# Second layer of a hybrid decoder: weights times values in fp32 on two column tiles of TensorE, instead of in high and low halves

## The chip, the cores and the metric

The kernel runs on one core of a Trainium2 chip. The metric is the device time of one execution in microseconds (us). The core's engines run side by side, each with its own instruction queue in program order: TensorE (PE; its weight loads are listed as PEld), VectorE (DVE), ScalarE (ACT), GpSimd (POOL) and SyncE (SP, which issues the DMAs here). L808 stands for line 808 of the kernel before.

## The reference

Two layers over x of shape (1, 1024, 1024) in float32. The first is differential attention, the second stick-breaking attention with 16 heads of 64; keys and values of the second are projected from the first one's output. The change touches the second layer's last einsum.

```python
def _stick_breaking(q, k, v):
    ...
        mask = kpos[None, :] < qpos[:, None]
        z = jnp.einsum('bhqd,bshd->bhqs', qb, k).astype(jnp.float32) * scale
        log_beta = jax.nn.log_sigmoid(z)
        log_1mb = jnp.where(mask, jax.nn.log_sigmoid(-z), 0.0)
        suffix = lax.cumsum(log_1mb, axis=3, reverse=True) - log_1mb
        a = jnp.where(mask, jnp.exp(log_beta + suffix), 0.0)
        return jnp.einsum('bhqs,bshe->bhqe', a.astype(v.dtype), v)

def _sb_layer(x, k, v, norm_g, w_in, w_out):
    ...
    o = _stick_breaking(q.reshape(b, s, SB_HEADS, SB_HEAD_DIM), k, v)
    o = o.reshape(b, s, SB_W) * jax.nn.silu(g)
    return x + o @ w_out
```

## The kernel before

Most matmuls take fp32r operands. To keep fp32 accuracy, an operand is split in a high half (an ACT copy to fp32r) and a low half (a DVE subtraction), and products of halves are summed in PSUM: three for the projections (`group`, L192 to L194) and for the scores (`scores`, L235).

The second layer works on eight pairs of heads. For a pair, `qkv_b` projects keys, values and queries with columns of both heads together; `v_done` (L745) has the values transposed back to rows (`v_rows`) and writes for each head j one 128 x 128 block for each block of 128 keys: 64 columns of high halves and 64 of low ones, in an order that puts the high ones on the columns of that head (L748 to L753). `unit_s_b` computes, for one block of 128 queries, the scores of both heads in two row tiles of the array (64 rows each, L235), evacuates them with ACT (L778), masks the diagonal block with POOL (L780) and runs the stick-breaking weights through ACT and DVE (L787 to L793), one row of queries for each partition.

`unit_t_b` takes a pair m of query blocks. Its steps (c, t) run over the heads c, and within a head over pairs t of key blocks, t = 0 to m. A step transposes the weights (`transposed`, L253: four 128 x 128 transposes into one PSUM tile `tr`, three in the last step t = m, where one block is masked away and its halves are zeroed by POOL, L267 and L268), splits the transposed weights in halves `th` (ACT, L269) and `tl` (DVE, L270), and multiplies each half of each of the two key blocks with the block of values (L808, L809), 256 query columns each. The sum of a head stands in PSUM in two sets of 64 partitions, weights times high values and weights times low ones. At the head's last step ACT copies the second set (L814) and DVE adds the first (L815) into `hd.o`. When both heads are through, `hd.done` counts the unit; `gate_mul` (L356) multiplies with the gate and stores to DRAM, and `OutProj` multiplies with the output weights.

The order of work: `run_layer` merges two lists of steps by the costs given with each step. The main list has the units of the current pair, with the T unit of one m behind the S unit of the next; the other has the projections of the next pair. The tile framework then orders the instructions of each engine by a simulated timeline (`schedule_with_timeline_sim=True`), so that instructions that would wait are passed by others that are ready. [...] SBUF tiles rotate by tags: three `th` and three `tl` in the pool of the whole kernel, four `v` of which a pair of the second layer holds two, eight score tiles `zl`, of which a unit with m of 2 or 3 holds four.

## Time and profile before

| | |
|---|---|
| median of 3 runs | 1470.85 us (1469.36 to 1471.21) |
| profiled execution | 1470.77 us |
| its span, first to last instruction | 1469.0 us |
| mean granted clock of TensorE | 0.98 |
| busy: PE, PEld, DVE, ACT, POOL | 96%, 81%, 74%, 64%, 20% |

The first layer and the first projections of the second run up to about 760 us, the second layer's attention with the projections of the following pairs from there to 1412 us, and the output projection closes the kernel. Busy times are those of one execution. Matmuls overlap in the pipeline, so the sum of their durations is more than PE's busy time; how far apart their starts are tells what one costs. [...]

### The profile page before, as it was taken

Reading aid. Unit: us, or ns where it says so; the run is one execution under the profiler, and the core shown is the slowest. Engines: PE = TensorE matmul, PEld = TensorE weight load, DVE = VectorE, ACT = ScalarE, POOL = GpSimd, SP = SyncE. Lnnn points to the kernel's source line nnn. Section 1 sums busy time; section 2 is a strip of 40 time slices with the busy share of each in tenths; the row PEclk is TensorE's granted clock in tenths of the full one; section 3 lists DMA queues with packets and bytes.
Section 4 is the critical chain, followed back from the end, with each engine's and each line's share of the span. In section 5 each row is a group of like instructions: output and inputs, shape, how many; then the busy total and the mean of one; then the engine's idle time right before and its main releaser. Section 6 shows DMA issues by size and latency. Waiting matters only on the chain.

```text
span 1469.0 us, 24503 instructions
## 1 busy us (share of the span) xinstructions
PE 1414.9 (96%) x8944; PEld 1192.0 (81%) x8944; DVE 1088.0 (74%) x2251; ACT 943.5 (64%) x1940; POOL 288.2 (20%) x545
## 2 busy tenths in 40 slices
PE   8999999999999999999999998998989999988899
PEld 7888888888888888799877776777867777767699
DVE  7586777777776867875458786887878788889952
ACT  7555566656565655453468777787777887788720
POOL 0111212121212112100011321322333242323100
PEclk9999999999999999999999998999999999998899
DMA  5111111111111124623111110111101010233412
GB/s 202 58 30 44 44 44 44 44 44 44 44 44 44 44 72 173 215 94 108 58 58 30 35 53 29 51 37 44 43 8 51 30 58 29 91 111 125 177 72 80
DMA packets 43113, 99.40 MB, mean 68 GB/s; under 512 B 4848, under 2 KB 6640, under 8 KB 41968
## 3 DMA queue, kind: packets, MB, share of 16 engines
q1 hardware_dynamic: 42992, 97.83, 19.4%
q8 instruction: 71, 1.16, 0.3%
q14 instruction: 50, 0.41, 0.1%
HBM read 74.74 MB, written 23.07 MB: 67 GB/s over the span
## 4 chain that ended last, share of the span: by engine, by line
PE 76%; DVE 12%; ACT 5%; issue 4%; DMA 1%; POOL 0%; SPq 0%; ACTq 0%; DVEq 0%; POOLq 0%
PE proj L192 18%; PE proj L193 18%; PE proj L194 17%; PE sc L235 8%; PE tr L263 5%; DVE u4k L792 5%; DVE u4k L790 2%; PE av L808 2%; PE av L809 2%; DVE tl L270 1%; PE av L638 1%; PE av L640 1%; PE av L639 1%; ACT u4k L788 1%; PE tr L571 1%
## 5 line engine op out<-in xcount | busy, mean ns | idle before, releaser
L192 PE MATMUL proj<-ah,w 128*128 128x512 f32 x768 | 310.3, 404 | 4.1 <-DVE kl L243 4.1
L193 PE MATMUL proj<-al,w 128*128 128x512 f32 x768 | 309.8, 403 | 0.0
L194 PE MATMUL proj<-ah,w 128*128 128x512 f32 x768 | 308.9, 402 | 0.0
L192 PE MATMUL proj<-w,ah 128*128 128x256 f32 x992 | 289.8, 292 | 4.0 <-DVE v L422 1.9
L194 PE MATMUL proj<-w,al 128*128 128x256 f32 x992 | 285.0, 287 | 0.0
L193 PE MATMUL proj<-w,ah 128*128 128x256 f32 x992 | 284.8, 287 | 0.0
L192 PEld LDWEIGHTS proj<-w,ah 128*128 128x128 f32 x992 | 191.3, 193 | 15.2 <-issue 5.8
L193 PEld LDWEIGHTS proj<-w,ah 128*128 128x128 f32 x992 | 191.5, 193 | 2.3 <-issue 1.0
L194 PEld LDWEIGHTS proj<-w,al 128*128 128x128 f32 x992 | 191.4, 193 | 1.5 <-issue 1.2
L192 PEld LDWEIGHTS proj<-ah,w 128*128 128x128 f32 x768 | 146.8, 191 | 39.8 <-DVE kl L243 5.6
L792 DVE TENSOR_TENSOR_SCAN u4k<-zl,u4k 128x768 f32<-128x768 f32 (+4 forms) x96 | 175.0, 1828 | 0.9
L193 PEld LDWEIGHTS proj<-al,w 128*128 128x128 f32 x768 | 146.9, 191 | 35.0 <-issue 7.1
L194 PEld LDWEIGHTS proj<-ah,w 128*128 128x128 f32 x768 | 146.5, 191 | 32.1 <-issue 3.0
L235 PE MATMUL sc<-kh,q 64*128 64x512 f32 (+2 forms) x768 | 159.7, 399 | 11.0 <-ACT zl L778 10.4
L270 DVE TENSOR_TENSOR tl<-tr,th 128x512 fp32r<-128x512 f32 (+1 forms) x240 | 146.5, 629 | 29.8 <-ACT th L269 28.6
L269 ACT ACTIVATE th<-tr 128x512 fp32r<-128x512 f32 (+1 forms) x240 | 126.2, 554 | 37.2 <-PE tr L263 32.1
L263 PE MATMUL tr<-ident,zl 128*128 128x128 f32 x864 | 131.0, 277 | 10.7 <-ACT zl L793 6.1
L793 ACT ACTIVATE zl<-u4k 128x768 f32<-128x768 f32 (+4 forms) x96 | 81.1, 846 | 87.9 <-DVE u4k L792 74.0
L161 ACT ACTIVATE w<-raw,cols 128x256 fp32r<-128x256 f32 x240 | 104.6, 502 | 46.6 <-PE proj L193 31.5
L780 POOL TENSOR_SCALAR_AFFINE_SELECT zl<-zl 128x128 f32<-128x128 f32 (+1 forms) x96 | 78.1, 819 | 278.9 <-ACT zl L778 278.7
L790 DVE SCALAR_TENSOR_TENSOR u4k<-zl,u4k 128x768 f32<-128x768 f32 (+4 forms) x96 | 95.5, 1007 | 44.9 <-ACT u4k L789 44.8
L235 PEld LDWEIGHTS sc<-kh,q 64*128 64x128 f32 x768 | 76.2, 186 | 62.7 <-issue 17.9
(148 smaller groups left out, 2630.7 us busy)
## 6 DMA issues: line engine op xcount, KB each, us to landing
raw<-in_w_kv_dram SPq DMA_DIRECT2D x32, 256.0 KB, 2.7
raw<-in_w_b_dram SPq DMA_DIRECT2D x32, 256.0 KB, 2.7
raw<-in_w_qk_dram SPq DMA_DIRECT2D x28, 256.0 KB, 2.7
raw<-in_w_vg_dram SPq DMA_DIRECT2D x28, 256.0 KB, 2.9
og_a<-o SPq DMA_DIRECT2D x28, 256.0 KB, 2.0
og_b<-o SPq DMA_DIRECT2D x28, 256.0 KB, 2.0
raw<-in_a_w_out_dram SPq DMA_DIRECT2D x26, 256.0 KB, 2.8
raw<-in_b_w_out_dram SPq DMA_DIRECT2D x26, 256.0 KB, 2.7
```

The lines of the kernel that those rows point to most:

```text
L161: act.activation(h[:, i], r, AF.Copy, scale=g)
L192: pe.matmul(box["p"], lh, rh, start=(j == 0), stop=False)
L193: pe.matmul(box["p"], lh, rl, start=False, stop=False)
L194: pe.matmul(box["p"], ll, rh, start=False, stop=last)
L235: pe.matmul(pts[:, c, :wm], q[a][HI[c], rs_], k[b][HI[c], off:off + wm], start=(a + b == 0), stop=(a == 1))
L263: pe.transpose(pt[:, o:o + P], a[:, (2 * t + b) * P:(2 * t + b + 1) * P], ident)
L269: act.activation(th[:, skip:], pt[:, skip:], AF.Copy)
L270: dve.tensor_tensor(tl[:, skip:], pt[:, skip:], f32(th[:, skip:]), ALU.subtract)
L780: pool.affine_select(t3[:, :, n - P:], t3[:, :, n - P:], [[0, len(cs)], [-1, P]], ALU.is_ge, -BIG, base=-1, channel_multiplier=1)
L790: dve.scalar_tensor_tensor(u, zc, 0.0, u, ALU.min, ALU.subtract)
L792: dve.tensor_tensor_scan(ur, t[:, 1:w2 + 1][:, ::-1], ur, 0.0, ALU.add, ALU.subtract)
L793: act.activation(zc, u, AF.Exp, scale=-1.0)
```

## The change

In the second layer the transposed weights are no longer split. Each head gets one fp32 copy `tt` (head 0 by ACT, head 1 by DVE), and the values are kept as fp32 in one block of 128 columns for both heads. A step of `unit_t_b` now works on both heads: head c multiplies its 64 columns of values, as an fp32 matmul with 64 output columns, into partitions 64c to 64c + 63 of one `av` tile, in an array tile of 128 rows by 64 columns. The blocks are transposed in the order even, odd query block for the first key block and odd, even for the second, so that a step has for each head one matmul of 256 columns and two of 128 (one in the last step). Zeroing, halves and the addition of the two sets fall away; one DVE copy takes the result of both heads. The tiles `th`, `tl` move to the first layer's pool, `tt` (four buffers) lies in the second's; the values of a pair take one `v` tile in place of two. The step costs given to the merge have the same sum.

```diff
--- before.py
+++ after.py
@@ -261,8 +261,8 @@
                 o = (i * 2 + j) * P
                 if o >= skip:
                     pe.transpose(pt[:, o:o + P], a[:, (2 * t + b) * P:(2 * t + b + 1) * P], ident)
-        th = T("th", [P, HALF], B["th"], F32R)
-        tl = T("tl", [P, HALF], B["th"], F32R)
+        th = T("th", [P, HALF], B["th"], F32R, layer[0])
+        tl = T("tl", [P, HALF], B["th"], F32R, layer[0])
         if last:
             pool.memset(f32(th[:, :P]), 0.0)
             pool.memset(f32(tl[:, :P]), 0.0)
@@ -335,7 +335,11 @@
 
     def alloc_kv(hd):
         if hd.v is None:
-            hd.v = [T("v", [P, 4, 2, P], 4, F32R) for _ in range(2)]
+            if layer[1]:
+                v = T("v", [P, 8, P], 4)
+                hd.v = [v[:, 0:4], v[:, 4:8]]
+            else:
+                hd.v = [T("v", [P, 4, 2, P], 4, F32R) for _ in range(2)]
             hd.k = (T("kh", [P, S], 2, F32R), T("kl", [P, S], 2, F32R))
 
     def alloc_q(hd, hf):
@@ -744,13 +748,8 @@
 
         def v_done(hf, pt):
             tr = v_rows(pt)
-            t3 = tr.rearrange("p (r j e) -> p r j e", r=4, j=2)
-            for j in range(2):
-                hi = hd.v[hf][:, :, j, 64 * j:64 * j + 64]
-                lo = hd.v[hf][:, :, j, 64 - 64 * j:128 - 64 * j]
-                with hp():
-                    act.activation(hi, t3[:, :, j, :], AF.Copy)
-                    dve.tensor_tensor(lo, t3[:, :, j, :], f32(hi), ALU.subtract)
+            with hp():
+                act.activation(hd.v[hf].rearrange("p r e -> p (r e)"), tr, AF.Copy)
 
         def proj(done):
             return lambda W, hf: proj_t(W, xT2, hf, lambda pt: done(hf, pt))
@@ -799,24 +798,41 @@
         hd = heads_b[p]
         box = {}
 
-        def t_step(c, t):
-            if c == 0 and t == 0:
+        def t_step(t):
+            if t == 0:
                 box["p"] = PS("av", B["av"])
-            pc = box["p"][:, c * 256:c * 256 + 256]
-            for i, (kb, th, tl) in enumerate(transposed(hd.at[2 * m][c], hd.at[2 * m + 1][c], t, t == m)):
-                vt = hd.v[kb // 4][:, kb % 4, c, :]
-                pe.matmul(pc, vt, th, start=(t + i == 0), stop=False)
-                pe.matmul(pc, vt, tl, start=False, stop=(t + i == m + 1))
-            if t == m:
-                hi = slice(64 * c, 64 * c + 64)
-                lo = slice(64 - 64 * c, 128 - 64 * c)
-                oc = hd.o[m // 2][hi, (m % 2) * 256:(m % 2) * 256 + 256]
-                act.activation(oc, pc[lo, :], AF.Copy)
-                dve.tensor_tensor(oc, pc[hi, :], oc, ALU.add)
-                if c == 1:
-                    hd.done[m // 2] += 1
-
-        return [(4 * 55 + 4 * 109, lambda c=c, t=t: t_step(c, t)) for c in range(2) for t in range(m + 1)]
+            po = box["p"][:, :256]
+
+            last = t == m
+            at = []
+            for c in range(2):
+                ae, ao = hd.at[2 * m][c], hd.at[2 * m + 1][c]
+                pt = PS("tr", B["tr"])
+                n = HALF - P if last else HALF
+                for i, (a, b) in enumerate(((ae, 0), (ao, 0), (ao, 1), (ae, 1))[:n // P]):
+                    pe.transpose(pt[:, i * P:(i + 1) * P], a[:, (2 * t + b) * P:(2 * t + b + 1) * P], ident)
+                tt = T("tt", [P, HALF], 4, pool=layer[0])
+                if c == 0:
+                    act.activation(tt[:, :n], pt[:, :n], AF.Copy)
+                else:
+                    dve.tensor_copy(tt[:, :n], pt[:, :n])
+                at.append(tt)
+            for c in range(2):
+                vt = hd.v[t // 2][:, 2 * (t % 2), HI[c]]
+                pe.matmul(po[HI[c], :], vt, at[c][:, 0:256], start=(t == 0), stop=False)
+            for c in range(2):
+                vt = hd.v[t // 2][:, 2 * (t % 2) + 1, HI[c]]
+                if last:
+                    pe.matmul(po[HI[c], P:256], vt, at[c][:, 256:384], start=False, stop=True)
+                else:
+                    pe.matmul(po[HI[c], P:256], vt, at[c][:, 256:384], start=False, stop=False)
+                    pe.matmul(po[HI[c], 0:P], vt, at[c][:, 384:512], start=False, stop=False)
+            if last:
+                oc = hd.o[m // 2][:, (m % 2) * 256:(m % 2) * 256 + 256]
+                dve.tensor_copy(oc, po)
+                hd.done[m // 2] += 1
+
+        return [(8 * 55 + 4 * 109 * 2, lambda t=t: t_step(t)) for t in range(m + 1)]
 
     def sink_b(rb, t, cs):
         nc.sync.dma_start(out[0, rb * P:(rb + 1) * P, cs[0]:cs[1]], t[:, cs[0]:cs[1]])
```

## Rows read from the trace of the kernel before

**Rows 1.** The page, chain that ended last: share by engine.

```profile
PE 76%; DVE 12%; ACT 5%; issue 4%; DMA 1%; POOL 0%; SPq 0%; ACTq 0%; DVEq 0%; POOLq 0%
```

**Rows 2.** Stretches: length, busy PE, PEld, DVE, ACT, POOL, PEclk, DMA, GB/s.

```profile
760.00:880.00 120.00, 120.00 (x650) 94.36 (x649) 93.45 (x131) 92.42 (x166) 27.02 (x57) 1.00 0.11 36
880.00:1300.00 420.00, 396.30 (x2146) 311.19 (x2144) 344.37 (x470) 324.02 (x594) 120.81 (x231) 0.96 0.14 46
1300.00:1400.00 100.00, 82.72 (x556) 70.76 (x555) 92.17 (x131) 78.63 (x139) 26.13 (x62) 0.90 0.37 132
```

**Rows 3.** Waits of PE, 880 to 1400: total us, times, longest us.

```profile
PE sc L235 <- ACT zl L778: 10.4, 9, 2.7
PE av L809 <- DVE tl L270: 7.0, 9, 2.8
PE tr L263 <- ACT zl L793: 6.1, 7, 2.3
```

**Rows 4.** Timeline of PE, end of a run: start, duration, instruction.

```profile
...
900.88 0.28 PE L808 MATMUL av<-th,v 128*128 128x256 f32 x1
901.00 0.28 PE L809 MATMUL av<-tl,v 128*128 128x256 f32 x1
```

**Rows 5.** PE timeline, then groups (busy us, mean ns): fp32 matmul.

```profile
86.69 0.59 PE L645 MATMUL tr<-t1k,ones 128*128 128x256 f32 x2
...
L645 PE MATMUL tr<-t1k,ones 128*128 128x256 f32 x64 | 19.5, 385 | 0.0
```

**Rows 6.** Timeline of PE: scores in row tiles between full-array matmuls.

```profile
...
918.20 0.28 PE L808 MATMUL av<-th,v 128*128 128x256 f32 x1
918.32 0.28 PE L809 MATMUL av<-tl,v 128*128 128x256 f32 x1
918.53 0.50 PE L235 MATMUL sc<-kh,q 64*128 64x512 f32 x2
918.87 0.40 PE L235 MATMUL sc<-kl,q 64*128 64x512 f32 x2
919.10 0.40 PE L235 MATMUL sc<-kh,q 64*128 64x512 f32 x2
919.43 0.50 PE L194 MATMUL proj<-ah,w 128*128 128x512 f32 x1
919.77 0.39 PE L192 MATMUL proj<-ah,w 128*128 128x512 f32 x1
```

**Rows 7.** Timeline of PEld over the same scores.

```profile
...
918.53 0.19 PEld L235 LDWEIGHTS sc<-kh,q 64*128 64x128 f32 x2
918.64 0.19 PEld L235 LDWEIGHTS sc<-kl,q 64*128 64x128 f32 x2
```

**Rows 8.** Groups by line and shape: busy us, mean ns, idle before.

```profile
...
L270 DVE TENSOR_TENSOR tl<-tr,th 128x512 fp32r<-128x512 f32 x144 | 96.3, 682 | 10.3 <-ACT th L269 9.3
...
L808 PE MATMUL av<-th,v 128*128 128x256 f32 x320 | 90.4, 304 | 4.5 <-DVE o L815 3.8 <-ACT th L269 0.3
...
L269 ACT ACTIVATE th<-tr 128x512 fp32r<-128x512 f32 x144 | 82.5, 595 | 28.4 <-PE tr L263 25.7 <-PE av L808 1.5
...
L270 DVE TENSOR_TENSOR tl<-tr,th 128x384 fp32r<-128x384 f32 x96 | 52.2, 548 | 19.5 <-ACT th L269 19.3
...
L269 ACT ACTIVATE th<-tr 128x384 fp32r<-128x384 f32 x96 | 46.8, 492 | 8.9 <-PE tr L263 6.5 <-PE av L808 2.1
...
L815 DVE TENSOR_TENSOR o<-av,o 64x256 f32<-64x256 f32 x64 | 26.7, 417 | 19.0 <-ACT o L814 18.0
...
L814 ACT ACTIVATE o<-av 64x256 f32<-64x256 f32 x64 | 24.2, 378 | 22.0 <-PE av L809 20.7
...
L267 POOL MEMSET th<- 128x128 f32 x96 | 20.7, 215 | 239.5 <-PE av L639 92.5 <-PE av L808 72.1 <-DVE small L116 32.9
...
L753 DVE TENSOR_TENSOR v<-tr,v 128x256 fp32r<-128x256 f32 x32 | 13.3, 416 | 11.0 <-ACT v L752 10.9
...
L357 DVE CAST o<-o 128x512 fp32r<-128x512 f32 x28 | 13.2, 471 | 4.3 <-POOL o L356 4.2
...
```

## The prediction

> **What bounds the kernel now.** I read the chain of work that ended last first: TensorE (PE) holds 76% of it, VectorE (DVE) 12%, ScalarE (ACT) 5% [rows 1]. That is a mean over two different regimes, so the stretches come next [rows 2]. From 760 to 880 us PE is busy for the whole 120 us at a granted clock of 1.00, although DVE is busy 93.45 us (78%) and ACT 92.42 us (77%): there PE alone sets the time. From 880 to 1300 PE idles 420 - 396.30 = 23.7 us, its clock has a mean of 0.96, and DVE is busy 82%. From 1300 to 1400, where the last head pair has little projection work beside it, PE idles 17.3 us, the clock is 0.90, and DVE is busy 92%.
>
> The time that PE loses in the second layer is therefore the idle 41.0 us, plus the clock. [...] Together at most 68 us: 40.5 before 1300 and 27.3 behind it. That is all that relief for DVE and ACT can give back. Who PE waits for is in the waits from 880 to 1400 [rows 3]: scores for ACT's evacuation L778 (10.4 us), weights times values for the low halves L270 (7.0), transposes for ACT's last exponential L793 (6.1). Only the second is removed directly; the other two wait because ACT and DVE are in-order queues with the removed work in them.
>
> **The change part by part: matmuls.** A step of `unit_t_b` handles 256 keys of one query pair m. Per head pair the four m have 1+2+3+4 = 10 such steps, 4 of them last ones (t = m); over eight pairs 48 full and 32 last steps. Before, each has four 256-column matmuls for each of two heads, 80 x 8 = 640, which agrees with the 320 of L808 and as many of L809 [rows 8]. They follow one another at 0.12 us [rows 4], so the part removed is 640 x 0.12 = 76.8 us.
>
> The trace has an fp32 matmul of the same width: L645, 256 columns of fp32. It appears as two records, each with its own weight load; both together last 0.59 us where one lasts 0.385 [rows 5], so the second starts some 0.21 us behind the first. [...] TensorE comes out even only if the two heads' column tiles really run side by side.
>
> No column tile runs in the trace before. The nearest rows are the row tiles of the scores: two 512-column matmuls of the two heads last 0.40 us together where one alone would take that, and the next pair starts 0.23 us later [rows 6]: so tiles on separate parts of the array do run beside each other. Their weight loads come ahead of the waiting matmuls (loads of the kl pair at 918.64, its matmuls at 918.87) [rows 6, 7]. But matmuls start in program order, and there the heads alternate. Here, the two passes of head 0 come before those of head 1. With u = 0.215 us for a 256-column pass: head 0 first pass 0 to u; its second u to 2u, head 1's first beside it; head 1's second 2u to 3u, beside it both passes of head 0's first 128-column matmul. In a full step head 0 then has its other 128-column matmul (two halves of u), beside whose second pass only the first of head 1's four starts; the other three follow alone. Sum 5.5u = 1.18 us; a last step, with one 128-column matmul for each head, is 4u = 0.86. Without any overlap they are 8u = 1.72 and 6u = 1.29; with perfect overlap 4u = 0.86 and 3u = 0.645.
>
> Entering the row tiles moves the first start from 0.12 to 0.21 us behind the last full-array matmul, and leaving them moves the next start from 0.23 to 0.33 [rows 6]: 0.19 us for both. I price the column tiles alike, once for each step: 80 x 0.19 = 15.2 us (0 if such changes cost nothing, some 30 if the planner puts projections between the heads).
>
> Forecast for PE: 48 x 1.18 + 32 x 0.86 + 15.2 - 76.8 = +22.6 us. No overlap: 82.6 + 41.3 + 15.2 - 76.8 = +62.3. Perfect overlap: 41.3 + 20.6 + 15.2 - 76.8 = +0.3. I take the first, because the row tiles overlap and the order of the passes is fixed by the code. On every reading PE gets nothing back: the gain, if any, is in the stalls.
>
> [...]
>
> **Copies.** The transposes stay as many (four, or three in a last step, for each head). Before, each head's step has an ACT copy (L269) and behind it a DVE subtraction (L270). In the second layer these are 96 full and 64 last ones, two thirds of the counts in [rows 8]; the rest is the first layer's. ACT keeps head 0's only: 48 x 0.595 + 32 x 0.492 = 44.3 us less [rows 8]. DVE turns from 96 x 0.682 + 64 x 0.548 = 100.5 us to 80 plain copies out of PSUM. A DVE copy of that shape is not in the trace; the dearest reading is the subtraction's own price (same source and width), 50.2 us, the cheapest the 0.471 us of the copy L357 within SBUF, 80 x 0.471 = 37.7. I take 50.2, the row that reads PSUM; so 50.3 us less, to 62.8. The copy for head 1 no longer waits for ACT, so the two run side by side.
>
> The result: 64 ACT copies L814 (24.2 us) fall away, and 64 DVE additions L815 of 256 columns become 32 copies as wide on both heads' partitions: 32 x 0.417 = 13.3 us less [rows 8]. This copy waits for the last matmul of both heads, and the scan and the softplus steps of the next block are queued behind it on DVE; before, the addition waited for ACT as well, so the wait gets shorter. The gate L356 on POOL and the next unit's first matmul (one `av` buffer) wait for it, as they did.
>
> The values: the 32 DVE subtractions L753 (13.3 us) fall away; on ACT the same elements are copied in half as many instructions, which I cost at nothing. The zeroing of half tiles on POOL falls away, 128 x 0.215 = 27.5 us, but POOL was waiting most of the time. No DMA is added or moved. Half as many value buffers are held for each head. In units m = 2 and 3 head 0's score tiles come free later, with head 1's; eight buffers against four of a unit cover that, and if they did not, the next unit's scores would wait for about one more step, 1 to 2 us.
>
> Sum: DVE 50.3 + 13.3 + 13.3 = 76.9 us less, ACT 44.3 + 24.2 = 68.5 less, PE 22.6 more.
>
> **What the relief gives back.** Spread over the 640 us from 760 to 1400, DVE loses 0.12 us and ACT 0.107 us in each us. From 880 to 1300 that leaves DVE 344.37 - 50 = 294 us and ACT 324.02 - 45 = 279 us of about 405, 73% and 69%: both below the 78% and 77% at which PE never idles from 760 to 880 [rows 2]. All 40.5 us could then go; I take three quarters, 30, because the longest waits in [rows 3] are on L778 and L793, which remain. From 1300 to 1400 DVE falls from 92 to 80 us, still the busiest after PE, so that only about what it loses is gained: 14 of 27.3, an estimate with the shorter copy chain in it. Together 44 us.
>
> Net 22.6 - 44 = -21.4 us: the span goes from 1469.0 to 1447.6. The profiled execution took 1470.77 us, 1.8 more than its span and 0.08 below the median of 1470.85; so 1449 us.
>
> **The rivals.** *The tiles take turns.* The second head's passes start only when the first head's have ended. PE is then 62.3 us longer; a busier PE fills more of its stalls, say 50 of 68: +12, 1483 us. It decides the sign as soon as PE's addition is over what the stalls give, at 44 us that is 0.55 us for a step. For it: no row shows fp32 on column tiles. Against: the row tiles' 0.23 us for a pair.
> *The stalls stay.* Relief goes into other waits of the ACT and DVE chain, and only the waits on L270 and L815 and their low clock go, about 18 us: +4.6, 1475 us. For it: L778 and L793 lead [rows 3]. Against: 760 to 880.
> *Full overlap.* The planner, which orders instructions by a simulated timeline, brings the heads' matmuls together so that their passes alternate: +0.3 - 44, 1427 us.
> [...]
>
> **How the numbers follow.** Forecast 0.52, turns 0.19, stalls stay 0.12, full overlap 0.13, bare loads 0.04. The forecast's own range is 1425 (all 68 us given back) to 1465. For eight in ten I take 1424 to 1484: it takes in full overlap, stalls that stay and most of the turns. About 0.2% (3 us) is what a measurement of this kernel can tell from no change. Forecast and full overlap are nearly all faster; of turns and stays I give a sixth to faster and a fifth to no difference: faster 0.68, same 0.08, slower 0.24.
>
> **What would show it.** In the timeline of PE the first pass of head 1 should start within 0.01 us of head 0's second pass; a full step should take about 1.2 us, a last one 0.9, between its first matmul and the next full-array one. L269's successor should be 80 ACT copies, DVE busy 77 us less, PE idle below 15 us from 880 to 1300 with a clock near 1.00. The prediction is wrong if steps take 1.7 us, if PE idles as before with DVE below 75%, or if the planner splits steps so that array changes number far above 80.

## The result, and the profile after

The changed kernel takes **1481.76 us** (median of 4 runs, 1479.62 to 1482.37) where the kernel before takes 1470.59 beside it (4 runs): a ratio of 1.0074, with a 95% interval of 1.0057 to 1.0092. So the change costs 11.2 us; the forecast was 21.4 us less.

The page after answers to [rows 1]; the first line is busy time by engine, the second the chain of work that ended last, by engine. Line numbers are those of the kernel that a view shows; L792 of the changed kernel is L793 of the kernel before.

```profile
PE 1427.4 (96%) x9136; PEld 1162.2 (79%) x9136; DVE 1025.6 (69%) x2107; ACT 884.1 (60%) x1780; POOL 262.4 (18%) x417
PE 87%; DVE 5%; ACT 3%; issue 2%; DMA 1%; POOL 1%; SPq 0%; POOLq 0%; DVEq 0%; ACTq 0%
```

The removed copies are really gone from DVE and ACT, and DVE's share of the chain fell from 12% to 5%. TensorE's rose from 76% to 87%. The same three stretches as [rows 2], from the table of busy time by stretch (stretch, length, busy time of PE, PEld, DVE, ACT and POOL with the number of instructions, granted clock, DMA share, GB/s):

```profile
760.00:880.00 120.00, 120.00 (x660) 88.35 (x659) 80.15 (x103) 81.43 (x137) 24.17 (x38) 1.00 0.11 36
880.00:1300.00 420.00, 393.22 (x2224) 283.82 (x2224) 299.76 (x375) 282.19 (x486) 103.56 (x150) 0.96 0.13 45
1300.00:1400.00 100.00, 91.22 (x637) 73.18 (x636) 77.29 (x105) 61.33 (x102) 22.28 (x36) 0.95 0.35 122
```

From 880 to 1300 us DVE now is busy 71% and ACT 67%, down from 82% and 77%, and yet TensorE idles 420 - 393.22 = 26.8 us, more than the 23.7 of before, at the same clock of 0.96. In the last stretch it idles 8.8 us in place of 17.3. To compare the whole of the second layer, take each kernel from 760 us to its end. Before:

```profile
760.00:1469.00 709.00, 664.34 (x3884) 540.67 (x3882) 554.58 (x778) 504.94 (x915) 174.66 (x353) 0.96 0.17 60
```

and after:

```profile
760.00:1480.20 720.20, 676.98 (x4088) 511.04 (x4086) 494.79 (x640) 446.33 (x758) 151.11 (x227) 0.96 0.17 59
```

TensorE is busy 12.6 us longer and idle 43.2 us where it was 44.7. Some 2.9 us of the 12.6 came before: the last L642 of the first layer starts at 653.7, its counterpart L638 at 650.8, with the same instructions. That is not the change: in the kernels below this matmul starts anywhere from 649.3 to 653.7, and here the granted clock stood at its lower level for 10.2 us up to then, in the kernel before for 3.4. That leaves 9.7 us of added busy time and 1.4 us less of idle time.

Busy time holds the clock, too. The clock records of the two traces have two levels, 1.00 and 0.50. The clock stood at the lower one for 54.6 us from 760 us on before, with TensorE busy in 44.5 of them, and for 52.0 us after, busy in 32.9. The projections' matmuls of 512 columns (L192 to L194) start 0.427 us apart at the lower level and 0.228 at the upper (medians of 43 and 1148 in the trace before). If matmuls take twice as long there (an estimate from the two levels; these two medians give 1.87 times), the low clock adds 22.2 us to the busy time before and 16.4 after, 5.8 less. At the full clock the added matmul work is then 15.5 us. So the 11.2 us are 2.9 from ahead of the change and **15.5 of added matmul work, less 1.4 of idle time and some 5.8 of low clock given back**, where 22.6 and 44 had been forecast; the 44 were idle time and clock together.

The waits of TensorE from 760 to 1440 us (line < what it waited for: us in all, times, longest) answer to [rows 3]; the last line is of the kernel before, over the same stretch:

```profile
PE tr L813 <- ACT zl L792: 14.1, 8, 3.3
PE proj L192 <- DVE kl L243: 10.5, 5, 4.5
PE sc L235 <- ACT zl L777: 7.0, 4, 3.4
PE proj L192 <- DVE kl L426: 4.2, 1, 4.2
...
PE av L822 <- DVE tt L818: 0.8, 1, 0.8
...
PE proj L192 <- DVE kl L243: 4.1, 3, 3.0
```

The waits on the low halves are gone, as they had to be; on the new copies TensorE waits 0.8 us. But the waits on ACT's last exponential (L792, 14.1 us for 6.1) and on projections whose PSUM bank DVE has not emptied (L243, 10.5 for 4.1) have grown by about as much as went.

### The profile page after: what moved, and what is told of

The parts are those of the page before. It is cut to its first block, busy times and chain, and to the rows that moved or that the text cites. A ratio compares the mean times of both kernels' runs of the same rounds, so it can differ in the third digit from the quotient of the medians.

```text
span 1480.2 us, 24248 instructions
## 1 busy us (share of the span) xinstructions
PE 1427.4 (96%) x9136; PEld 1162.2 (79%) x9136; DVE 1025.6 (69%) x2107; ACT 884.1 (60%) x1780; POOL 262.4 (18%) x417
## 4 chain that ended last, share of the span: by engine, by line
PE 87%; DVE 5%; ACT 3%; issue 2%; DMA 1%; POOL 1%; SPq 0%; POOLq 0%; DVEq 0%; ACTq 0%
PE proj L192 20%; PE proj L193 20%; PE proj L194 19%; PE sc L235 9%; PE tr L813 5%; PE av L822 4%; PE tr L263 2%; DVE u4k L791 2%; PE av L642 1%; PE av L644 1%; PE av L643 1%; DVE u4k L789 1%; PE tr L279 1%; PE tr L575 1%; PE tr L649 1%
## 5 line engine op out<-in xcount | busy, mean ns | idle before, releaser
L192 PE MATMUL proj<-ah,w 128*128 128x512 f32 x768 | 311.2, 405 | 10.5 <-DVE kl L243 10.5
L194 PE MATMUL proj<-ah,w 128*128 128x512 f32 x768 | 308.5, 402 | 0.0
L192 PE MATMUL proj<-w,ah 128*128 128x256 f32 x992 | 290.2, 293 | 10.0 <-DVE kl L426 5.0
L194 PE MATMUL proj<-w,al 128*128 128x256 f32 x992 | 285.0, 287 | 0.0
L192 PEld LDWEIGHTS proj<-w,ah 128*128 128x128 f32 x992 | 191.2, 193 | 21.9 <-issue 6.0
L194 PEld LDWEIGHTS proj<-w,al 128*128 128x128 f32 x992 | 191.0, 193 | 2.1 <-issue 1.6
L192 PEld LDWEIGHTS proj<-ah,w 128*128 128x128 f32 x768 | 146.5, 191 | 48.4 <-DVE kl L243 12.1
L791 DVE TENSOR_TENSOR_SCAN u4k<-zl,u4k 128x768 f32<-128x768 f32 (+4 forms) x96 | 171.6, 1796 | 0.8
L194 PEld LDWEIGHTS proj<-ah,w 128*128 128x128 f32 x768 | 146.5, 191 | 30.7 <-issue 2.4
L235 PE MATMUL sc<-kh,q 64*128 64x512 f32 (+2 forms) x768 | 155.2, 395 | 7.5 <-ACT zl L777 7.0
L792 ACT ACTIVATE zl<-u4k 128x768 f32<-128x768 f32 (+4 forms) x96 | 81.0, 844 | 97.6 <-DVE u4k L791 82.0
L162 DVE SCALAR_TENSOR_TENSOR w<-raw,cols,w 128x256 fp32r<-128x256 f32 x240 | 106.8, 492 | 29.8 <-ACT w L161 28.9
L622 ACT ACTIVATE zl<-zl,small 128x256 f32<-128x256 f32 (+7 forms) x128 | 98.3, 769 | 43.5 <-DVE small L621 27.7
L613 DVE CUSTOM_DVE_ANT_0 zl<-sc,mask_a 128x384 f32<-128x384 f32 (+3 forms) x192 | 99.8, 552 | 33.8 <-PE sc L235 33.1
L777 ACT ACTIVATE zl<-sc 128x512 f32<-128x512 f32 (+4 forms) x160 | 81.9, 548 | 67.6 <-PE sc L235 57.9
```

What stands on the lines that cost most here:

```text
L162: dve.scalar_tensor_tensor(l[:, i], r, g, f32(h[:, i]), ALU.mult, ALU.subtract)
L192: pe.matmul(box["p"], lh, rh, start=(j == 0), stop=False)
L194: pe.matmul(box["p"], ll, rh, start=False, stop=last)
L235: pe.matmul(pts[:, c, :wm], q[a][HI[c], rs_], k[b][HI[c], off:off + wm], start=(a + b == 0), stop=(a == 1))
L613: dve.tensor_tensor_reduce(p[c][:, off:off + w], pts[:, c, :w], mask, 1.0, BIG, ALU.add, ALU.min, mn[c][:, k:k + 1])
L622: act.activation(p[c][:, :n], p[c][:, :n], AF.Exp, bias=b, scale=-1.0, accum_out=s[:, c:c + 1])
```

## How long a step takes

The timeline of TensorE shows the new steps (start, duration, engine, line, operation, tiles, shape, count in a row of the same kind):

```profile
902.55 0.39 PE L192 MATMUL proj<-ah,w 128*128 128x512 f32 x1
902.87 0.65 PE L822 MATMUL av<-tt,v 128*64 128x256 f32 x2
903.45 0.55 PE L813 MATMUL tr<-ident,zl 128*128 128x128 f32 x3
903.75 0.48 PE L193 MATMUL proj<-al,w 128*128 128x512 f32 x1
904.16 0.43 PE L822 MATMUL av<-tt,v 128*64 128x256 f32 x1
904.16 0.43 PE L828 MATMUL av<-tt,v 128*64 128x128 f32 x2
...
909.16 0.65 PE L822 MATMUL av<-tt,v 128*64 128x256 f32 x4
909.62 0.42 PE L826 MATMUL av<-tt,v 128*64 128x128 f32 x4
909.97 0.50 PE L235 MATMUL sc<-kh,q 64*128 64x512 f32 x2
```

At 904.16 one head's 256-column pass (L822) and the other head's 128-column passes (L828) start at the same time: fp32 matmuls on two column tiles do run beside each other. At 909.16 stands a whole last step, four records of 256 columns and four of 128, and 0.81 us later (909.97) the next matmul starts. The step at 902.87 is another thing: the two passes of head 0's L822 stand alone, the next instruction starts 0.58 us later, and the rest of that step follows at 904.16 behind transposes and a projection. No late copy forced this on the chip: head 1's copy had ended at 898.73 + 0.69 = 899.42 us.

```profile
898.73 0.69 DVE L818 COPY tt<-tr 128x512 f32<-128x512 f32 x1 [1.70 <-PE tr L813]
```

The cut stands in the order that the planner gave the instructions. Sorted by the order of their passes, only 24 of the 80 steps (10 full ones, 14 last ones) have both heads together; in the other 56 head 0's L822 comes earlier. In 23 of those it stands beside the matmuls of another step and costs nothing (18 stretches of one step's rest and the next one's head 0 take 1.065 us each, a whole step 1.070). In 33 it stands alone, and then a full step takes 1.59 us in all (0.58 + 1.01), a last one 1.37 (0.58 + 0.79). The expectation of the step in one block counts 32 cut steps, by the lengths alone. Stretches of these matmuls with nothing else between them are called runs here; the changed kernel has 109.

## The experiments

Two explanations stood against each other from the start: matmul time (steps cost more than they should), and stalls that are not made by the load of DVE and ACT and so don't answer to relief. The letters in the quoted expectations name theories of that run; the text under each says which of the two its result speaks for. Each kernel ran beside the kernel before, at 1470.2 to 1472.2 us. Runs of different kernels that were not taken together are compared to no better than the 2 us by which these differ.

**Relief without the change.** The kernel before, with DVE's low half in the second layer left out: the weights' high half is multiplied twice, so the matmuls stay as many and the low part of the weights is missing from the output. The low half's zeroing on POOL goes, too.

```diff
...
-        dve.tensor_tensor(tl[:, skip:], pt[:, skip:], f32(th[:, skip:]), ALU.subtract)
+        if layer[1]:
+            tl = th
+        else:
+            dve.tensor_tensor(tl[:, skip:], pt[:, skip:], f32(th[:, skip:]), ALU.subtract)
```

> The kernel before, with the second layer's low halves of the weights left out: L270 is not done there and the high half is multiplied twice, so PE has the same matmuls while DVE loses about 100 us (160 subtractions) and POOL 14 us. The result lacks the products with the low halves. Theory A (the stalls stand once for each head pair, where the next pair's projections begin, and the copies are not what PE waits for there): only the waits on L270 and their low clock go, 10 to 16 us, 1455 to 1461 us. Theory B (stalls go with the load of DVE, as forecast): 30 to 45 us less, 1425 to 1440.

Measured: 1463.92 us, ratio 0.9948 (0.9931 to 0.9966). From 760 us to the end:

```profile
760.00:1462.70 702.70, 657.62 (x3890) 537.20 (x3888) 466.89 (x619) 504.95 (x915) 163.95 (x290) 0.96 0.17 60
```

DVE is busy 87.7 us less, more than the whole change takes from it, and TensorE idles 702.70 - 657.62 = 45.1 us, as before (44.7). The 6.3 us gained are busy time of TensorE, 6.7 less. Relief of DVE alone gives back no stall; ACT keeps its copies in this kernel.

**The copies back.** The changed kernel, each transposed tile copied a second time, by the other engine, into a tile that nobody reads.

```diff
+                dead = T("dead", [P, HALF], 1, pool=layer[0])
+                if c == 0:
+                    dve.tensor_copy(dead[:, :n], pt[:, :n])
+                else:
+                    act.activation(dead[:, :n], pt[:, :n], AF.Copy)
```

> The changed kernel with the removed copies put back as dead work: each step's PSUM tile is also copied by the other engine into a scratch tile that nobody reads (80 ACT and 80 DVE copies more, about 44 and 45 us), the matmuls unchanged. Theory A: at most a few us more than the changed kernel, 1480 to 1488. Theory B: the stalls that the relief took away come back, half of the removed load being there again: 1500 or more.

Measured: 1499.47 us, ratio 1.0190 (1.0169 to 1.0211), 17.7 above the changed kernel; TensorE idles 53.4 us (10.2 more) and is busy 684.53 (7.5 more). DVE is busy 43.6 us more and ACT 37.3, where the change had taken 59.8 and 58.6 in this stretch. So the load is not without effect: this part of it is worth up to 18 us under the order of the changed kernel (by the code the dead copy also holds the transposes' PSUM bank, which is in this number). Against the kernel before, whose instructions the planner ordered otherwise, no gain of that size is seen.

**Fewer matmuls in a step.** The transposes in another order, so that the second key block too is one matmul of 256 columns.

```diff
-                for i, (a, b) in enumerate(((ae, 0), (ao, 0), (ao, 1), (ae, 1))[:n // P]):
+                for i, (a, b) in enumerate((((ae, 0), (ao, 0), (ao, 1)) if last else ((ae, 0), (ao, 0), (ae, 1), (ao, 1)))[:n // P]):
...
-                    pe.matmul(po[HI[c], P:256], vt, at[c][:, 256:384], start=False, stop=False)
-                    pe.matmul(po[HI[c], 0:P], vt, at[c][:, 384:512], start=False, stop=False)
+                    pe.matmul(po[HI[c], :], vt, at[c][:, 256:512], start=False, stop=False)
```

> The changed kernel with the second key block transposed in the order even, odd, so that a full step has two 256-column matmuls for each head instead of one of 256 and two of 128. If the passes of the two heads overlap only as far as the program order lets them, a full step is 5 passes of 0.215 us in place of 5.5: 48 x 0.107 = 5.2 us less, 1476.5; with fewer loads and less to interleave perhaps 1474. If PE's V part does not set the time, no difference: 1481.

Measured: 1486.49 us, ratio 1.0103 (1.0084 to 1.0123). The expectation of a gain fell: TensorE is busy 684.3 us from 760 on, 7.3 more, and the planner broke these matmuls into 119 runs where the changed kernel has 109.

**The heads together.** A dependency by hand makes head 0's first matmul wait for head 1's copy too, so that both are ready when the step begins.

```diff
-                    dve.tensor_copy(tt[:, :n], pt[:, :n])
+                    copy = dve.tensor_copy(tt[:, :n], pt[:, :n])
...
-                pe.matmul(po[HI[c], :], vt, at[c][:, 0:256], start=(t == 0), stop=False)
+                mm = pe.matmul(po[HI[c], :], vt, at[c][:, 0:256], start=(t == 0), stop=False)
+                if c == 0:
+                    tc.add_manual_dep(mm.ins, copy.ins.name, ...)
```

> The changed kernel with one dependency more in each step: the first matmul of head 0 also waits for the copy of head 1, so that the planner no longer sends one head's two passes ahead and the rest later (76 runs of these matmuls on PE in place of 109). Binding the steps as a block cost a stop at each of them, so its 1591 us said nothing on the cuts; here there is no stop but this one wait. Theory C (cut steps are what PE pays for): 16 us of PE go, 1464 to 1470. If the stalls set the time and PE's work in the second layer does not: 1478 to 1484.

Measured: 1465.17 us, ratio 0.9956 (0.9937 to 0.9975): 16.6 us below the changed kernel with the same work on every engine, and now below the kernel before. From 760 us to the end:

```profile
760.00:1463.40 703.40, 654.63 (x4077) 504.05 (x4075) 490.14 (x638) 442.84 (x757) 146.19 (x225) 0.96 0.18 60
```

TensorE is busy 22.4 us less than in the changed kernel (some 2.5 of it before the change's place: its last L642 starts at 651.2), in 76 runs. A whole full step, in its timeline:

```profile
1144.60 0.34 PE L235 MATMUL sc<-kh,q 64*128 64x384 f32 x2
1144.87 0.65 PE L822 MATMUL av<-tt,v 128*64 128x256 f32 x4
1145.35 0.44 PE L830 MATMUL av<-tt,v 128*64 128x128 f32 x4
1145.57 0.44 PE L831 MATMUL av<-tt,v 128*64 128x128 f32 x4
1145.94 0.55 PE L813 MATMUL tr<-ident,zl 128*128 128x128 f32 x3
```

It takes 1145.94 - 1144.87 = 1.07 us, and all 48 full steps and 32 last ones now stand whole. From the first start of each run to the next other matmul, at the full clock, these matmuls add up to 76.4 us where the changed kernel has 94.5; and 33 entries fewer into the column tiles, 0.09 us each (worked out below), make 3 us more. Together 21 us, where TensorE's busy time fell by 19.9 behind the first layer. The matmul side is settled by it. But TensorE idles 703.40 - 654.63 = 48.8 us, 5.6 more than in the changed kernel and 4.1 more than before the change: the stalls are not touched, and 16.6 us in all are left.

**A step in one block.** The same by another means: the step's matmuls in a section that nothing may enter.

```diff
+            with tc.tile_critical():
+                for c in range(2):
+                    vt = hd.v[t // 2][:, 2 * (t % 2), HI[c]]
...
```

> The changed kernel with the matmuls of one step bound together for the planner, so that nothing comes between them (79 runs of them on PE in place of 109; the work is the same). In the changed kernel 32 of the steps are cut: one head's two passes stand alone (0.58 us) and the rest elsewhere (1.01 or 0.79 us), 1.59 and 1.37 us together where a whole step takes 1.07 and 0.80. Theory C (the rise comes from cut steps): about 17 cuts of full steps by 0.52 and 14 of last ones by 0.57 go, 17 us less, 1465 us. If the time is set by the stalls at the change of pairs alone: the PE time saved is lost again in longer stalls, 1478 to 1482.

Measured: 1590.79 us, ratio 1.0812. The cuts are gone (79 runs), but TensorE idles 124.9 us from 760 on and its clock has a mean of 0.90: the section stops more than it holds together. It says nothing for or against either explanation.

**Where the stall stands.** Along the trace the stall is not spread: it returns at each change of head pairs, every 84 us or so (in the changed kernel at about 913, 1001, 1085, 1164, 1250 and 1332 us). One of them, in the kernel with the heads together. TensorE (in brackets how long it was idle before and what ended that):

```profile
1150.25 0.40 PE L235 MATMUL sc<-kh,q 64*128 64x512 f32 x2
1154.03 0.47 PE L813 MATMUL tr<-ident,zl 128*128 128x128 f32 x1 [3.38 <-ACT zl L792]
1156.70 0.80 PE L192 MATMUL proj<-ah,w 128*128 128x512 f32 x1 [2.20 <-DVE kl L243]
```

ACT in the same time:

```profile
1150.56 1.15 ACT L213 ACTIVATE o<-o 128x512 f32<-128x512 f32 x2
1153.24 0.74 ACT L792 ACTIVATE zl<-u4k 128x640 f32<-128x640 f32 x1 [1.53 <-DVE u4k L791]
1153.88 1.06 ACT L241 ACTIVATE kh<-proj 128x512 fp32r<-128x512 f32 x2
1154.84 1.08 ACT L777 ACTIVATE zl<-sc 128x512 f32<-128x512 f32 x2
```

and DVE:

```profile
1150.59 3.93 DVE L791 TENSOR_TENSOR_SCAN u4k<-zl,u4k 128x640 f32<-128x640 f32 x2
1154.45 0.66 DVE L214 SCALAR_TENSOR_TENSOR o<-g2k,o 128x512 f32<-128x512 f32 x1
```

TensorE starts nothing between 1150.65 and 1154.03. ACT's exponential L792 waits for DVE's scan, itself idle for 1.53 us; behind L792 in ACT's queue stand the copies L241, which empties a projection's bank, and L777, which empties the scores' banks. The scores that L777 reads were written by 1150.65 and the projection that L241 reads before 1144 (no other stands on TensorE until 1156.70), and TensorE needs both banks; yet both copies start only behind L792, in the order of the queue. TensorE and ACT wait for DVE, whose mean load here is 70%: it is the scan that they wait for, not DVE's time. In the changed kernel, some 9 us ahead of such a stall, DVE waits 4.61 us and ACT 5.06 us for TensorE (at 904.03 and 906.06 in its timelines). So first TensorE has work and the others none, then the reverse.

Four kernels tried to take out what meets there. The gate's softplus chain of the second layer (silu, L211 to L216) left out, the gate then being the plain projection, in the changed kernel and in the kernel before:

```diff
     def silu(pg, u):
+        if layer[1]:
+            with hp():
+                act.activation(u, pg, AF.Copy)
+            return
```

> The changed kernel with the second layer's SiLU left out (the gate is one ACT copy out of PSUM, so the result lacks the SiLU): 16 times three ACT and two DVE instructions and one of POOL less, about 30 us of ACT, 18 of DVE, 24 of POOL, all of them queued at the change from one head pair to the next. Theory A: the stalls there, some 5 us and the low clock behind them for each of seven pairs, shrink by half or more: 1450 to 1465. Theory B: a load of 48 us on two engines is a third of what the change removed for some 12 us of stalls: 4 us less, 1477.

> The kernel before without the second layer's SiLU, as in e5_no_silu (the result lacks the SiLU). There the changed kernel lost 35 us of 1481.8, 32 of them stalls of PE. If the stalls are the same ones in both kernels, 25 to 38 us go here too, 1433 to 1446, and the copies were never in them. If the copies of the kernel before fill the time that the SiLU leaves: 5 to 15 us less, 1455 to 1465.

Measured: 1446.74 us (ratio 0.9835), 35.0 below the changed kernel, with TensorE idle 19.6 us and a clock of 0.99; and 1451.30 (0.9852), 20.9 below the kernel before, idle 37.3. Without that work the two can't be told apart: their ratios, 0.9835 (0.9816 to 0.9853) and 0.9852 (0.9832 to 0.9873), overlap. Is it where the work lies, or that it is there? The same work, put off to after the second and third unit of a pair:

```diff
+        if layer[1]:
+            deferred.append(lambda: silu_rest(g, u))
...
+                if i in (1, 2):
+                    main.append((0.0, lambda: deferred and deferred.pop(0)()))
```

> The changed kernel with the second layer's SiLU moved, not removed: behind its copy out of PSUM, its five remaining instructions for each half are issued one and two units later, in the middle of the next pair's units. Theory A (what counts is what stands in the queues of ACT and DVE at the change of pairs): most of the 35 us that leaving the SiLU out gave, 1450 to 1465. Theory B (the load as such): the same as the changed kernel, 1478 to 1485.

> The kernel before with the same move of the SiLU. Theory A: its stalls at the change of pairs are as long (41 us idle in the second layer, and the low clock), so it gains as much, 1440 to 1458. If the stalls of the kernel before come from the copies that the change removes: 1465 to 1471.

Measured: 1487.64 us (ratio 1.0115) and 1477.29 (1.0045), each about 6 us above its own parent. The move did not clear the place, though. In the changed kernel the two halves' L214 stand at 997.26 and 1000.80 us, around the stall; in the kernel with the move (L226) they stand as follows, up to the same change of pairs (DVE, the last row TensorE):

```profile
963.25 0.68 DVE L226 SCALAR_TENSOR_TENSOR o<-g2k,o 128x512 f32<-128x512 f32 x1
...
991.47 0.69 DVE L226 SCALAR_TENSOR_TENSOR o<-g2k,o 128x512 f32<-128x512 f32 x1
...
996.25 0.43 DVE L373 CAST o<-o 128x512 fp32r<-128x512 f32 x1 [2.29 <-POOL o L372]
996.60 1.28 DVE L255 TENSOR_TENSOR kl<-proj,kh 128x512 fp32r<-128x512 f32 x2
997.34 0.79 PE L192 MATMUL proj<-ah,w 128*128 128x512 f32 x1 [2.09 <-DVE kl L255]
```

One half went to the middle of the pair. The other came only some 6 us ahead of the change of pairs, and the gate's products on POOL stayed there: DVE waits 2.29 us for one of them, with the copy behind it in the queue that TensorE waits for. So moving one half takes nothing from the time; whether the gate's place makes the stall is not settled by this.

**Values first, and more lead.** The projection of values ahead of that of keys (in this kernel the two exchange their weights as well, so its output is another one; the work is as much):

```diff
         def v_done(hf, pt):
+            alloc_kv(hd)
...
-        return [(lambda: w_pair(w_kv[p], cols[:, 16:24]), [proj(k_done), proj(v_done)]),
+        return [(lambda: w_pair(w_kv[p], cols[:, 16:24]), [proj(v_done), proj(k_done)]),
```

> The changed kernel with each pair's values projected ahead of its keys. The longest waits of PE at the change of pairs (10.5 us in 5 waits) are for the low half of the keys to leave its PSUM bank, queued on DVE behind the last scans and the gate; the values leave theirs with one ACT copy. Theory A in its narrow form (that one wait sets the stall): 10 us less and some low clock, 1466 to 1474. If the queues as a whole are late, PE waits for the next thing: 1478 to 1485.

Measured: 1486.29 us, 1.0106. And the lead that the merge gives the attention's steps over the projections of the next pair, 0.1 and 0.3 for 0.02 (only this place of the line is shown):

```diff
- ... "leada": 0.02, "leadb": 0.02, ...
+ ... "leada": 0.02, "leadb": 0.1, ...
```

> The changed kernel with the attention's steps sent ahead of the next pair's projections by 10% of a pair in place of 2% (the same instructions, in another order). In the changed kernel ACT and DVE stand idle for 5 us just ahead of each stall of PE, waiting for PE, which does projections. Theory D (the stalls come from the order, the load of ACT and DVE no longer decides): several us either way, most likely less, 1465 to 1478. If the order is not it: 1480 to 1484.

> As the last, with 30% of a pair. Theory D: again another time by some us, 1460 to 1490, the better of the two showing which way the order should go. If the order is not it: 1480 to 1484.

Measured: 1482.56 us (1.0062) and 1495.09 (1.0155), TensorE idle 43.5 and 52.0. None of the three takes the stall away.

**POOL beside DVE.** The heads together, and the two products of the gate (L360, L362) on DVE instead of POOL in the second layer.

```diff
-            pool.tensor_tensor(o, o, hd.sg[hf], ALU.mult)
+            eng = dve if layer[1] else pool
+            eng.tensor_tensor(o, o, hd.sg[hf], ALU.mult)
...
-            pool.tensor_tensor(o.bitcast(F32R), o, f32(hi), ALU.subtract)
+            eng.tensor_tensor(o.bitcast(F32R), o, f32(hi), ALU.subtract)
```

> e14_heads_together with the two gate products of each half that POOL does in the second layer (the multiplication and the subtraction, 28 in all) done by DVE, same result. At the change of pairs PE waits for ACT's last exponential, behind which the evacuations of scores and keys are queued; it waits for a DVE scan of 640 columns that took 2.6 us beside the POOL product, 1.5 elsewhere. Theory E (it is POOL's products beside the scans that make DVE late there): the seven stalls lose about 1.1 us and some low clock each though DVE has 19 us more to do, 1450 to 1460. If DVE is simply full there: 1466 to 1475.

Measured: 1457.79 us, ratio 0.9914 (0.9894 to 0.9934), 7.4 below the heads together (6.2 by the two ratios): more work for DVE, and less time. What speaks for a cause is under the hardware below. The heads together with whole blocks of 256 columns, beside the same runs of the kernel before:

> e14_heads_together with the second key block in one 256-column matmul for each head, as in e4_whole_blocks, which came out 5 us slower than the changed kernel with more cuts (119 runs for 109). Without cuts: a full step was 1.01 us there against 1.07 at best, 48 x 0.05 = 2.6 us less, 1462 to 1465. If the planner's order for this form is worse by itself: 1468 or more.

Measured: 1458.77 us, ratio 0.9909 (0.9888 to 0.9931), 6.4 below. The edit that cost 4.7 us alone gains once its steps stay whole. A full step takes 1.015 us where it took 1.070, which is 48 x 0.055 = 2.6 us, as expected; the rest of the 6.4 is not matmul work, and its cause is open. (The profiled execution, at 1454.24 us the fastest of the four, flatters this kernel.)

**The order of the units.** The units of a pair run over m in the order 1, 3, 0, 2. The heads together with 2, 3, 1, 0 and with 2, 0, 3, 1 (one number at the end of line 46 picks the order):

```diff
- ... "ob": 2}
+ ... "ob": 10}
```

> e14_heads_together with the units of a pair in the order 2, 3, 1, 0 instead of 1, 3, 0, 2: the last unit of a pair is then the smallest (128 and 256 keys) and not one of 640 and 768. Theory F (the stall of each pair is the chain of its last unit, with no projections to fill PE): the stalls change with the order by more than 15 us, either way; if the end of the pair alone counts, they shrink, 1440 to 1455. If the stalls are made by load, not by place: 1460 to 1470.

> The same with the order 2, 0, 3, 1, whose last unit has 384 and 512 keys, both heads in one tile. Theory F: between the two others, 1450 to 1465, or again off by more than 15 us. By load: 1460 to 1470.

Measured: **1439.88 us**, ratio 0.9788 (0.9771 to 0.9805), and 1494.17, ratio 1.0152. One number is worth 54 us. The first of them from 760 us to the end:

```profile
760.00:1437.70 677.70, 648.23 (x4082) 501.88 (x4080) 493.97 (x639) 445.80 (x756) 152.10 (x225) 0.98 0.19 63
```

TensorE idles 29.5 us where it idled 48.8, with the same instructions on every engine. Is that the order alone? The kernel before in the same order:

> The kernel before with the order of units 2, 3, 1, 0, under which the heads-together form of the change took 1440 us. If the relief of the copies is worth little and the order much, the kernel before gains like it: 1440 to 1452. If ACT and DVE with the copies in them can't keep up in that order, so that the change's relief is what the order needs: 1460 to 1475, and the difference of some 25 us to the changed form is the relief that the forecast had looked for (44 us).

Measured: 1482.14 us, ratio 1.0073 (1.0054 to 1.0091).

```profile
760.00:1479.70 719.70, 660.06 (x3869) 540.42 (x3867) 561.09 (x776) 506.80 (x911) 172.85 (x353) 0.95 0.17 59
```

Here TensorE idles 59.6 us, and its waits name what the change removes:

```profile
PE tr L263 <- DVE tl L270: 15.4, 7, 6.1
PE av L809 <- DVE tl L270: 10.5, 10, 2.2
PE sc L235 <- ACT zl L778: 8.4, 7, 2.6
PE av L808 <- DVE o L815: 4.6, 5, 2.3
```

In the order 2, 3, 1, 0 the change (heads together) is worth 1482.14 - 1439.88 = 42.3 us: 30.2 of idle time and 11.8 of busy time, which holds the clock, 0.98 for 0.95 (beside each of the two the kernel before took 1471.4). In the order 1, 3, 0, 2 it is worth 6.5 (by the ratio of 0.9956; its interval gives 4 to 9). The relief is there, and in these two orders it is the order that decides whether TensorE gets it.

**All together.** Heads together, whole blocks, order 2, 3, 1, 0, gate products on DVE:

> The changed kernel with both heads together, the second key block whole, the order 2, 3, 1, 0, and the gate products on DVE. If the single gains add up (7 for DVE, 6 for whole blocks on 1440): 1427 us; if the new order has already taken the stalls that the gate products held: 1436 to 1442.

Measured: **1435.08 us**, ratio 0.9755 (0.9731 to 0.9779). It beats both kernels, the changed one by 46.7 us.

## Why the prediction failed, point by point

From -21.4 to +11.2 are 32.6 us: 36.8 of stalls and low clock that were not given back (44 - 1.4 - 5.8), 7.1 that the matmuls cost less than forecast (22.6 - 15.5), and 2.9 from ahead of the second layer (36.8 - 7.1 + 2.9 = 32.6).

**The failing step: what the relief gives back.** The step reasoned from mean load: at 78% and 77% TensorE doesn't idle, so below that it will not. After the change DVE and ACT stood at 71% and 67% from 880 to 1300, and it idled 26.8 us in place of 23.7. The 44 us came as 1.4 of idle time and some 5.8 of clock. A mean load says that the work fits, not that it arrives in time: the stall shown above is a chain through the queues of DVE, ACT and TensorE at the change of pairs, and shortening work elsewhere leaves it. The kernel before with 88 us less on DVE shows it by itself (idle 45.1), the pair of orders shows the other side (42.3 us gained where the waits are on the removed instructions, 6.5 where they are not). The waits had said so [rows 3]: 16.5 of the listed us were on L778 and L793, and the forecast took three quarters of everything all the same. The rival "stalls stay" counted 18 us, idle time and clock; even that was too much. Of the 68 us that the step started from, some 27 are the clock of [rows 2], as if the share that a stretch's mean lacks were lost in all of it (0.04 x 420 + 0.10 x 100). No run shows a loss of that size: before the change TensorE was busy in 44.5 us of the lower level from 760 us on, and 22.2 of them are lost by the estimate above.

**Matmuls: three terms were off, and they nearly cancel.** The price of a pass was not one of them: u = 0.215 us agrees with the trace before, where the second record of L645 starts 0.220 us behind the first (median of 32) and the next transpose 0.215 behind the second (L263, 11 cases). One head's fp32 matmul of 256 columns is thus 0.435 us where its two on halves were 0.24 at the spacing of [rows 4]. Overlap of the column tiles was forecast and found; the limit by program order, 5.5u and 4u, was not; that passes start only in the order of the code was the author's assumption. A whole full step takes 1.07 us up to the next other matmul, a last one 0.80. The way in comes on top: the first pass starts 0.32 us behind the last projection (902.55 to 902.87), where two projections stand 0.23 apart, so 0.09. That makes 1.16 and 0.89 us with the changes of the array, against 1.37 and 1.05 forecast, and against 1.05 and 0.84 for perfect overlap (4u + 0.19, 3u + 0.19). The code gives both passes of a head in one matmul, and still the four records at 1144.87 start in pairs, two there and two from 1145.14.

The removed matmuls were priced too low. The 0.12 us of [rows 4] is the spacing within a run; where scores follow, the kernel before has

```profile
896.69 0.38 PE L808 MATMUL av<-th,v 128*128 128x256 f32 x1
897.01 0.43 PE L235 MATMUL sc<-kl,q 64*128 64x384 f32 x1
```

0.32 us apart. Over the 597 of the 640 that the trace has at the full clock and without a wait behind them, the mean from one start to the next matmul's is 0.136 us: 87 us removed, not 76.8.

The whole steps are 48 x 1.16 + 32 x 0.89 = 84.2 us, and the cuts 21: 84.2 + 21 - 87 = +18, where 15.5 us of added work were measured at the full clock. For the heads together the same sum is 84.2 - 87 = -3, and its busy time at the full clock, reckoned as above, is 5 us below the kernel before. So the steps cost less than forecast (84 us for 99.4), what they replace cost 10 us more, and the cuts took most of that back.

**Array changes.** 80 were priced, "some 30 us if the planner puts projections between the heads"; there were 109 runs. The mechanism stood in the text, with 15 us more for it against the 21 that the cuts cost, and was given too small a weight.

**Copies.** Right. Groups by line of the changed kernel (count | busy us, mean ns | idle before and what ended it):

```profile
L818 DVE COPY tt<-tr 128x512 f32<-128x512 f32 x48 | 32.6, 683 | 21.9 <-PE tr L813 21.7
L818 DVE COPY tt<-tr 128x384 f32<-128x384 f32 x32 | 17.4, 545 | 30.0 <-PE tr L813 30.0
```

0.683 and 0.545 us are the subtraction's own price, as taken (0.682, 0.548). DVE's busy time fell by 62.4 us over the whole kernel where the sum was 76.9, ACT's by 59.4 (68.5). Neighbouring instructions that overlap do so by 0.08 us on DVE and 0.10 on ACT (medians in the trace before), so a busy time shrinks by less than the durations taken out; added up, the durations fell by 69.5 and 75.7 us. The last number of each row says the same as the waits: the copies wait for TensorE, not TensorE for them.

**The rivals.** "Tiles take turns" gave 1483 us and the time is 1481.76, by luck: the tiles don't take turns. That the time lies inside the range of 1424 to 1484 us is luck of the same kind, since that end of it was there for the turns. Bare loads, which have a chance of 0.04, are out: a full step has twelve weight loads of 0.136 to 0.139 us (the means of L822, L828 and L829), 1.6 us in all, and takes 1.07; each of the 832 loads of these matmuls in the changed kernel lies beside a running matmul. "Full overlap" was right on the matmuls in a whole step and took the 44 us with it. Among what would make the prediction wrong two of three things came: TensorE idle as before with DVE below 75%, and array changes far above 80.

**What stays open.** Why leaving out the gate's chain frees 35 us: moving it left half of it and its products near the stall, so place and load are not parted. Why the simulated timeline by which the planner orders the engines puts the chain of the stall where it does, and why the order 2, 3, 1, 0 suits the changed form. The change as it stands, without the added dependency, was not run in that order. Whether the kernel before has a better order too: only two were tried, 1470.6 and 1482.1 us. More buffers for `o`, and transposes one step ahead of their matmuls, were not tried.

## What to carry to other kernels

Count relief for an engine off the bound only at the place where the bound engine waits: list those waits, find the queue each stands in, and credit the edit with the ones whose own chain gets shorter; a mean load of 70% did not mean here that nothing waits. Where matmuls on separate tiles are meant to run side by side under a planner that orders the instructions itself, tie their start to the last of their inputs; otherwise it may put other work between them, and a half then runs alone. After such a change the old order of work is an order for another kernel: here one number moved the time by 54 us, and the change, with its heads together, gained 6.5 us in one order and 42 in another.

## What the runs showed of the hardware

Two fp32 matmuls on column tiles of 64 run beside each other: 1.07 us for twelve passes, of which four have 256 columns and eight 128; one after another they would take 8 x 0.215 = 1.72 us by the 0.215 us behind L645 in the trace before. A head alone takes 0.58 us for two passes of 256, with the way out of the tile in it.

In the changed kernel, a DVE instruction that reads and writes only SBUF lasted up to 1.1 us longer where it started during a product on POOL. From 760 us on, the five L214 that do so take 1.69 to 1.76 us, the nine others 0.68 (median). POOL (first fence) and DVE (second):

```profile
913.77 1.78 POOL L362 TENSOR_TENSOR o<-o,o 128x512 fp32r<-128x512 f32 x1 [0.54 <-DVE o L361]
916.84 1.72 POOL L216 TENSOR_TENSOR o<-g2k,o 128x512 f32<-128x512 f32 x1 [1.29 <-ACT o L215]
```

```profile
914.34 1.76 DVE L214 SCALAR_TENSOR_TENSOR o<-g2k,o 128x512 f32<-128x512 f32 x1
916.02 1.48 DVE L791 TENSOR_TENSOR_SCAN u4k<-zl,u4k 128x640 f32<-128x640 f32 x1
917.42 1.69 DVE L214 SCALAR_TENSOR_TENSOR o<-g2k,o 128x512 f32<-128x512 f32 x1
```

L214 alone takes 0.66 us (at 1154.45 above). Here it ends 0.55 us after POOL's product: 913.77 + 1.78 = 915.55 and 914.34 + 1.76 = 916.10, then 918.56 and 919.11. All five end 0.55 us after the product; why is not shown. An instruction that starts ahead of the product and runs into it is not longer: L791 at 916.02, with the product from 916.84, takes 1.48 us, as do seven such scans of 640 columns (median), against 1.49 in eight beside none. DVE instructions that read PSUM are not longer beside these products in the same trace: L243 takes 0.69 us in 6 cases beside one and 0.68 in 7 without; the copies L818 of 512 columns take 0.68 us in 3 cases beside one and in 45 without.

In the stall shown above the two scans take 3.93 us, and the first of them starts during this product on POOL. At 1.48 us for the second, as in the row at 916.02, the first takes some 2.5 (an estimate from these two numbers); in the changed kernel the scan at 1333.40, started during L362, takes 2.55. So the very chain that TensorE waits for is longer there:

```profile
1149.97 1.83 POOL L360 TENSOR_TENSOR o<-o,o 128x512 f32<-128x512 f32 x1
```

Moving two of the gate's three products away gave 7.4 us, with 40.2 us idle for 48.8; that fits, but the order of the instructions moved with it, so the cause of the gain is not shown alone.
